# Two-layer decoder trunk on one Trainium2 core: the low parts of the weight splits of the attention and output stages in one VectorE operation per unit in place of two

## The chip, the cores and the metric

The kernel runs on one core of one Trainium2 chip, in one launch. The metric is the device time in microseconds of that core; lower is better. Beside the plain runs there is one profiled execution, whose trace is read here. Engine names in the rows: PE is TensorE (matrix products and transposes), PEld its weight loads, DVE is VectorE, ACT is ScalarE, POOL is GpSimd, SP is SyncE, which issues most DMAs.

## The reference, cut to what matters

The input is x, 256 tokens by 1024, in float32, and goes through two layers. Each layer computes:

```
h = RMSNorm(x);  proj = h @ w_in          # aq ak av | ix | bq bk bv | gates
ya = sparse attention: an indexer (4 heads) scores the keys, each query keeps its top 64, 8 heads of 64
yb = differential attention: 4 heads, softmax1 - lambda * softmax2, RMS norm per head
x  = x + ( sigmoid(gA) * (ya @ w_up_a) + sigmoid(gB) * (yb @ w_up_b) ) @ w_out
x  = x + SwiGLU(RMSNorm(x))               # hidden width 2816
```

The output is x, 256 by 1024, float32.

## The kernel before, in words

Every large product is made with float32 accuracy from three products of a shorter type: a matrix is split into a high part (`wh` for weights, made by ScalarE, a copy into the type fp32r) and a low part (`wl`, made by VectorE, the raw weight minus the high part), and `mm3` (lines 237 to 242) issues high times high, high times low and low times high. In the rows these are the lines L240, L241 (the one that reads `wl`) and L242.

Weights come in units of 512 rows by 512 columns or the like, packed so that a unit is a tile of 128 partitions by 2048 numbers in two halves of 1024 (the unit `ix` of the indexer has 2 x 648). A layer has 34 units ahead of its main feed-forward part: gA0, ix, ak, aq, av, bk, gA1, bq, bv, gB0, uA, gB1, uB with two each (names as in `BLOCKS`), four of `wo`, and four of the first two slabs `fi0` and `fi1`. A unit's raw tile has 4 buffers, its high and its low tile 4 each (`RAWS`, `RING`).

`ensure(k)` is called just ahead of the first product that uses unit k, and splits all units up to it by `split_half`, half by half: ScalarE writes 1024 numbers of `wh` (L149), VectorE 1024 of `wl` (L150). A wait of a matmul on `wl` is on the half that it reads. The first four units of layer 0 call `split_half` directly in `first_block`; the feed-forward units after `fi1` go through `high` and `low` (L197, L201), where the low part of a unit is already one operation of 2048.

The order of TensorE's and GpSimd's instructions is the program's own. VectorE's and ScalarE's instructions between `early.close()` and the feed-forward part are put in order by the framework's scheduler, which works from its own estimate of each instruction's length; within an engine they then run strictly in that order. So a change of one operation can move others of that engine.

Names needed below. After the products of a block, VectorE makes the rotated queries and keys of 128 tokens (`rope`, L455, L456, L458; for attention A's keys first L471, with the factor `ak00r` that GpSimd makes in L273 and L276), and TensorE transposes them, four or three transposes of 128x128 (L249), some ticks later: `ak00T` is layer 0, tokens 0 to 127. For the indexer (`idx_finish`) the third transpose of `ix01T` reads a piece that VectorE copies last (L497). The top-64 search (`indexer`, L529 and L530) is eight rounds of a maximum and a replacement for each 128 queries, `sc00m` and `sc01m` in layer 0 and `sc10m` and `sc11m` in layer 1, and fills VectorE between the other work.

Of the kernel before, what the change touches and what calls it, by code (L numbers as in the profile page):

```python
# [10 lines left out]
F32 = mybir.dt.float32  # L11
F32R = mybir.dt.float32r
I32 = mybir.dt.int32
AF = mybir.ActivationFunctionType
ALU = mybir.AluOpType
# [71 lines left out]
def tile_trunk(ctx, tc, x, angle, wpk, widx, gnorm, gbias, gqk, dlam, subln, const, out):  # L87
    nc = tc.nc
# [21 lines left out]
    seq, uidx, where = [], {}, {}  # L110
# [8 lines left out]
    held, ready, split = {}, [], [0]  # L119

    def raw_of(u):
        if u not in held:
            src, w = where[u]
            name = "raw" + "".join(str(a) for a in u)
            if u[2] == "22":
                raw = pp.tile([P, 2048], F32, name=name, tag="yT", bufs=1)
            else:
                raw = wp.tile([P, 2048], F32, name=name, tag="raw", bufs=RAWS)[:, :2 * w]
            for j in range(2):
                nc.sync.dma_start(raw[:, j * w:j * w + w], src[j])  # L130
            held[u] = raw
        return held[u]

    def new_ready(i):
        assert len(ready) == i
        ready.append([wp.tile([P, 2048], F32R, name=f"w{h}{i}", tag="w" + h, bufs=RING) for h in "hl"])
        return ready[i]

    def split_half(parts=1, between=None):
        n = split[0]  # L140
        split[0] += 1
        i, j = divmod(n, 2)
        hi, lo = ready[i] if j else new_ready(i)
        raw = raw_of(seq[i])
        w = raw.shape[-1] // 2
        m = w // parts
        for k in range(parts):
            c = slice(j * w + k * m, j * w + (k + 1) * m)
            nc.scalar.activation(hi[:, c], raw[:, c], AF.Copy)  # L149
            nc.vector.tensor_tensor(lo[:, c], raw[:, c], hi[:, c].bitcast(F32), ALU.subtract)  # L150
            if k == 0 and between:
                between()

    def ensure(k):
        while split[0] < 2 * min(k + 1, len(seq)):
            split_half()


    stage = {}
# [52 lines left out]
    def unit(l, name, i, kc, w):  # L212
        u = uidx[(l, name, i)]
        ensure(u)
        return [a[:, :kc * w].rearrange("p (a b) -> p a b", a=kc) for a in ready[u]]
# [882 lines left out]
```

## Time and profile before

| | us |
|---|---|
| median of 3 runs | 762.66 |
| lowest, highest | 762.52, 764.41 |
| profiled execution, its own time | 762.28 |
| span of its trace | 760.5 |
| TensorE busy | 751.3 (99%) |
| VectorE busy | 573.6 (75%) |
| ScalarE busy | 470.6 (62%) |
| GpSimd busy | 108.7 (14%) |

The profiled execution's own time is 1.78 us more than the span from its first to its last instruction. A row of the timeline gives the start in us from the span's start, the duration, the engine, line, operation and tiles, how many instructions are merged in it, and in brackets the idle time ahead of it with what ended it. Matmuls overlap: a 128x512 one is shown with 0.39 us, but the next starts about 0.23 us after it. A late start is therefore read from the distance between starts; the bracket shows the part of it in which the engine had nothing left in its pipeline.

### The profile page before, as it was taken

The numbers are of one execution on the slowest core, as the hardware profiler recorded it, in microseconds if no ns is written. First come the engines' busy times: TensorE is split into PE (matmuls) and PEld (weight loads), VectorE is DVE, ScalarE is ACT, GpSimd is POOL, SyncE is SP. The second block draws the span as 40 slices with busy tenths as digits, with TensorE's granted clock in tenths as the row PEclk, the third lists the DMA queues.
The fourth block names the chain that finished last, engine by engine and source line by source line (L and its number), as shares of the span: only waits on it lengthen the run. The fifth ranks groups of instructions, "written<-read, shape, count | busy, mean of one in ns | idle before, by whom it ended". The sixth has DMA issues, their size and how long they took to land.

```text
span 760.5 us, 10268 instructions
## 1 busy us (share of the span) xinstructions
PE 751.3 (99%) x3638; PEld 617.0 (81%) x3638; DVE 573.6 (75%) x885; ACT 470.6 (62%) x938; POOL 108.7 (14%) x135
## 2 busy tenths in 40 slices
PE   8999999999999999999999999999999999999998
PEld 5877888888888888888888787888888888888886
DVE  5999757768777777777768987667777877787673
ACT  5766597655665656656547676876546666565660
POOL 5741220010031100010001411200002010000100
PEclk9999999999999999999999999999999999999999
DMA  9744635436568888977746273443476599868921
GB/s 317 290 168 166 235 125 183 162 115 234 206 167 264 234 275 258 275 231 221 240 150 221 91 242 125 177 170 125 166 272 213 152 218 293 255 236 270 231 102 55
DMA packets 45061, 154.60 MB, mean 203 GB/s; under 512 B 5409, under 2 KB 6177, under 8 KB 45010
## 3 DMA queue, kind: packets, MB, share of 16 engines
q1 hardware_dynamic: 40320, 136.97, 49.1%
q0 software_dynamic: 4688, 16.98, 12.7%
q8 instruction: 28, 0.46, 0.2%
q14 instruction: 23, 0.19, 0.1%
q10 hardware_dynamic: 2, 0.00, 0.0%
HBM read 152.89 MB, written 1.05 MB: 202 GB/s over the span
## 4 chain that ended last, share of the span: by engine, by line
PE 90%; DVE 5%; ACT 1%; DMA 1%; POOL 1%; issue 1%; SPq 0%; ACTq 0%; DVEq 0%
PE fo L242 5%; PE fo L240 5%; PE fo L241 5%; PE fi L242 5%; PE fi L241 5%; PE fi L240 5%; PE qX L242 3%; PE qX L240 3%; PE qX L241 3%; PE gB L240 2%; PE gB L242 2%; PE wo L242 2%; PE gB L241 2%; PE wo L240 2%; PE wo L241 2%; PE gA L240 2%
## 5 line engine op out<-in xcount | busy, mean ns | idle before, releaser
L240 PE MATMUL fo<-wh,aTh 128*128 128x512 f32 (+1 forms) x100 | 38.2, 382 | 0.0
L241 PE MATMUL fo<-wl,aTh 128*128 128x512 f32 (+1 forms) x100 | 38.1, 381 | 0.0
L242 PE MATMUL fo<-wh,aTl 128*128 128x512 f32 (+1 forms) x100 | 38.1, 381 | 0.0
L197 ACT ACTIVATE wh<-raw1q 128x1024 fp32r<-128x1024 f32 (+1 forms) x24 | 30.0, 1268 | 8.3 <-DMA raw1q<-wpk 7.0
L197 ACT ACTIVATE wh<-raw0q 128x1024 fp32r<-128x1024 f32 (+1 forms) x24 | 30.0, 1268 | 8.1 <-DMA raw0q<-wpk 5.6
L201 DVE TENSOR_TENSOR wl<-raw0q,wh 128x2048 fp32r<-128x2048 f32 x15 | 34.2, 2284 | 0.6 <-ACT wh L197 0.6
L201 DVE TENSOR_TENSOR wl<-raw1q,wh 128x2048 fp32r<-128x2048 f32 x15 | 34.2, 2284 | 0.6 <-ACT wh L197 0.6
L240 PE MATMUL fo<-wh,aT 128*128 128x512 f32 x80 | 32.0, 400 | 0.0
L240 PE MATMUL fi<-wh,f0Th 128*128 128x512 f32 x80 | 31.9, 399 | 0.0
L240 PE MATMUL fi<-wh,f1Th 128*128 128x512 f32 x80 | 31.9, 399 | 0.0
L242 PE MATMUL fo<-wh,aT 128*128 128x512 f32 x80 | 31.3, 391 | 0.0
L242 PE MATMUL fi<-wh,f1Tl 128*128 128x512 f32 x80 | 31.2, 391 | 0.0
L242 PE MATMUL fi<-wh,f0Tl 128*128 128x512 f32 x80 | 31.2, 390 | 0.0
L241 PE MATMUL fo<-wl,aT 128*128 128x512 f32 x80 | 31.2, 390 | 0.0
L241 PE MATMUL fi<-wl,f0Th 128*128 128x512 f32 x80 | 31.2, 390 | 0.0
L241 PE MATMUL fi<-wl,f1Th 128*128 128x512 f32 x80 | 31.2, 390 | 0.0
L201 DVE TENSOR_TENSOR wl<-raw1fo,wh 128x2048 fp32r<-128x2048 f32 x11 | 25.1, 2285 | 3.4 <-ACT wh L197 3.4
L201 DVE TENSOR_TENSOR wl<-raw0fo,wh 128x2048 fp32r<-128x2048 f32 x11 | 25.1, 2285 | 3.4 <-ACT wh L197 3.4
L197 ACT ACTIVATE wh<-raw0fo 128x1024 fp32r<-128x1024 f32 x22 | 22.0, 1050 | 7.9 <-issue 4.0
L197 ACT ACTIVATE wh<-raw1fo 128x1024 fp32r<-128x1024 f32 x22 | 22.0, 1049 | 7.6 <-issue 4.1
L240 PE MATMUL wo<-wh,mTh 128*128 128x512 f32 x64 | 25.6, 400 | 0.0
L242 PE MATMUL wo<-wh,mTl 128*128 128x512 f32 x64 | 25.0, 391 | 0.0
(1050 smaller groups left out, 2490.2 us busy)
## 6 DMA issues: line engine op xcount, KB each, us to landing
raw0q<-wpk SPq DMA_DIRECT2D x24, 512.0 KB, 6.0
raw1q<-wpk SPq DMA_DIRECT2D x24, 512.0 KB, 5.6
raw0fo<-wpk SPq DMA_DIRECT2D x22, 512.0 KB, 6.2
raw1fo<-wpk SPq DMA_DIRECT2D x22, 512.0 KB, 6.0
raw0fi<-wpk SPq DMA_DIRECT2D x20, 512.0 KB, 4.2
raw1fi<-wpk SPq DMA_DIRECT2D x20, 512.0 KB, 4.4
raw0q<-wpk POOLq DMA_DIRECT2D x12, 512.0 KB, 6.8
raw1q<-wpk POOLq DMA_DIRECT2D x12, 512.0 KB, 7.6
```

The costliest lines, as they stand in the source:

```text
L197: nc.scalar.activation(hi[:, k * w:k * w + w], raw[:, k * w:k * w + w], AF.Copy)
L201: nc.vector.tensor_tensor(ready[n][1], stage.pop(("raw", n)), ready[n][0].bitcast(F32), ALU.subtract)
L240: nc.tensor.matmul(acc, lhsT=sh, rhs=mh, start=first, stop=False, skip_group_check=more)
L241: nc.tensor.matmul(acc, lhsT=sh, rhs=ml, start=False, stop=False, skip_group_check=more)
L242: nc.tensor.matmul(acc, lhsT=sl, rhs=mh, start=False, stop=last, skip_group_check=more)
```

## The change

`ensure` no longer calls `split_half`. For each unit it now makes both high halves on ScalarE, as before in two operations of 1024, and then the whole low part in one VectorE operation of 2048 (1296 for `ix`). It applies to all units that go through `ensure`: 30 in layer 0 and 34 in layer 1. `split_half` stays for the first four units.

```diff
     def ensure(k):
+
         while split[0] < 2 * min(k + 1, len(seq)):
-            split_half()
+            n = split[0] // 2
+            split[0] += 2
+            hi, lo = new_ready(n)
+            raw = raw_of(seq[n])
+            w = raw.shape[-1] // 2
+            for j in range(2):
+                nc.scalar.activation(hi[:, j * w:j * w + w], raw[:, j * w:j * w + w], AF.Copy)
+            nc.vector.tensor_tensor(lo[:, :2 * w], raw, hi[:, :2 * w].bitcast(F32), ALU.subtract)
```

TensorE's and GpSimd's instructions stand in the same order as before. In the built program after, lines behind `ensure` have numbers higher by 8 (L458 is L466, L497 is L505), and the new operation is L164. Three places of VectorE's queue follow.

Layer 0, indexer, tokens 128 to 255: `ix01q` is the rotated indexer query and key, `wl<-raw0aq` are the low parts of the two units of aq, `ak00xn` the first step of the keys of attention A. Before:

```order
L456 TENSOR_TENSOR ix01kb<-ix01q,sg_271 128x64
L150 TENSOR_TENSOR wl_579<-raw0aq_580,wh_578 128x1024
L458 TENSOR_TENSOR ix01q<-ix01q,ix01kb 128x64
L150 TENSOR_TENSOR wl_606<-raw0aq_607,wh_605 128x1024
L497 COPY ix01q<-ix01q 128x64
L150 TENSOR_TENSOR wl_606<-raw0aq_607,wh_605 128x1024
L471 TENSOR_TENSOR ak00xn<-ak_382,ak00r 128x512
```

And now:

```order
L464 TENSOR_TENSOR ix01kb<-ix01q,sg_271 128x64
L164 TENSOR_TENSOR wl_603<-raw0aq_604,wh_602 128x2048
L466 TENSOR_TENSOR ix01q<-ix01q,ix01kb 128x64
L479 TENSOR_TENSOR ak00xn<-ak_382,ak00r 128x512
L505 COPY ix01q<-ix01q 128x64
```

The whole of a unit's low part stands ahead of the addition into `ix01q`, and `ak00xn`, which reads `ak00r` from GpSimd, has moved ahead of the copy.

Layer 0, queries of attention A, tokens 128 to 255 (`aq01q`), with the low part of bk's first unit. Before:

```order
L150 TENSOR_TENSOR wl_798<-raw0bk_799,wh_797 128x1024
L529 MAX sc01m_558<-nb_159 128x8
L474 TENSOR_SCALAR rqaq_163<-rqaq_163 128x8
L455 TENSOR_TENSOR aq01q<-aq_642,cg_270 128x512
L530 MATCH_REPLACE nb_159<-sc01m_558,nb_159 128x256
```

And now:

```order
L164 TENSOR_TENSOR wl_792<-raw0bk_793,wh_791 128x2048
L537 MAX sc01m_556<-nb_159 128x8
L482 TENSOR_SCALAR rqaq_163<-rqaq_163 128x8
L463 TENSOR_TENSOR aq01q<-aq_638,cg_270 128x512
L538 MATCH_REPLACE nb_159<-sc01m_556,nb_159 128x256
```

The neighbours are the same; the operation ahead of them has 2048 numbers in place of 1024, and the second half no longer follows behind `aq01q`.

Layer 1, queries of attention A, tokens 0 to 127 (`aq10q`), with av's second unit. Before:

```order
L525 SCALAR_TENSOR_TENSOR nb_3447<-sc11r_3807,iw_3445,nb_3447 128x256
L531 TENSOR_SCALAR nb_3446<-nb_3446 128x128
L529 MAX sc11m_3811<-nb_3447 128x8
L533 TENSOR_TENSOR nb_3446<-nb_3446,cst 128x128
L530 MATCH_REPLACE nb_3447<-sc11m_3811,nb_3447 128x256
L150 TENSOR_TENSOR wl_3978<-raw1av_3979,wh_3977 128x1024
L529 MAX sc11m_3814<-nb_3447 128x8
L474 TENSOR_SCALAR rqaq_3450<-rqaq_3450 128x8
L455 TENSOR_TENSOR aq10q<-aq_3836,cg_2058 128x512
```

And now:

```order
L164 TENSOR_TENSOR wl_3939<-raw1av_3940,wh_3938 128x2048
L537 MAX sc10m_3669<-nb_3416 128x8
L537 MAX sc11m_3775<-nb_3417 128x8
L538 MATCH_REPLACE nb_3416<-sc10m_3669,nb_3416 128x128
L538 MATCH_REPLACE nb_3417<-sc11m_3775,nb_3417 128x256
L539 TENSOR_SCALAR nb_3416<-nb_3416 128x128
L537 MAX sc11m_3778<-nb_3417 128x8
L541 TENSOR_TENSOR nb_3416<-nb_3416,cst 128x128
L538 MATCH_REPLACE nb_3417<-sc11m_3778,nb_3417 128x256
L482 TENSOR_SCALAR rqaq_3420<-rqaq_3420 128x8
L463 TENSOR_TENSOR aq10q<-aq_3800,cg_2032 128x512
```

Between the key rotation of this layer (`ak11xn`) and `aq10q` there now stand the whole low part, and of the search rounds two more maxima of `sc10m`, one more replacement of `sc10m` and one more of `sc11m` than before.

## Rows read from the trace of the kernel before

**Rows 1.** The page's span and its part on the engines: busy us, share of the span, count of instructions.

```profile
span 760.5 us, 10268 instructions
PE 751.3 (99%) x3638; PEld 617.0 (81%) x3638; DVE 573.6 (75%) x885; ACT 470.6 (62%) x938; POOL 108.7 (14%) x135
```

**Rows 2.** The view by stretches of time: length, busy us (and instructions) of PE, PEld, DVE, ACT, POOL, then the granted clock, the share of DMA and GB/s.

```profile
38.00:76.00 38.00, 36.93 (x183) 29.37 (x182) 37.35 (x101) 25.38 (x81) 10.16 (x8) 1.00 0.45 168
76.00:380.00 304.00, 304.00 (x1469) 250.40 (x1467) 226.55 (x303) 191.68 (x346) 33.14 (x41) 1.00 0.67 214
```

**Rows 3.** The timeline of TensorE at five places: unit ak (L241 reads `wl`), the indexer's transposes, and the transposes of aq01, aq10 and bk10, each with the row ahead of it.

```profile
29.45 0.39 PE L241 MATMUL ak<-wl,a0Th 128*128 128x512 f32 x1
...
33.31 0.39 PE L240 MATMUL ak<-wh,a0Th 128*128 128x512 f32 x1
34.08 0.50 PE L241 MATMUL ak<-wl,a0Th 128*128 128x512 f32 x1 [0.39 <-DVE wl L150]
...
35.34 0.49 PE L249 MATMUL ix00T<-cst,ix00q 128*128 128x128 f32 x3
35.59 0.48 PE L240 MATMUL ak<-wh,a0Th 128*128 128x512 f32 x1
...
38.43 0.38 PE L249 MATMUL ix01T<-cst,ix01q 128*128 128x128 f32 x2
39.75 0.33 PE L249 MATMUL ix01T<-cst,ix01q 128*128 128x128 f32 x1 [0.94 <-DVE ix01q L497]
...
65.05 0.39 PE L242 MATMUL av<-wh,a0Tl 128*128 128x512 f32 x1
65.57 0.63 PE L249 MATMUL aq01T<-cst,aq01q 128*128 128x128 f32 x4
...
431.86 0.39 PE L242 MATMUL av<-wh,a1Tl 128*128 128x512 f32 x1
433.04 0.63 PE L249 MATMUL aq10T<-cst,aq10q 128*128 128x128 f32 x4 [0.79 <-DVE aq10q L458]
...
457.90 0.66 PE L249 MATMUL bk10T<-cst,bk10q 128*128 128x128 f32 x4 [0.21 <-DVE bk10q L458]
```

**Rows 4.** The timeline of VectorE in layer 0, from ak's low parts to the keys of attention A.

```profile
26.80 2.96 DVE L150 TENSOR_TENSOR wl<-raw0ak,wh 128x1024 fp32r<-128x1024 f32 x2
...
29.76 1.48 DVE L150 TENSOR_TENSOR wl<-raw0ak,wh 128x1024 fp32r<-128x1024 f32 x1
31.16 0.41 DVE L455 TENSOR_TENSOR ix00q<-ix,plain 128x256 f32<-128x256 f32 x1
...
32.81 1.22 DVE L150 TENSOR_TENSOR wl<-raw0ak,wh 128x1024 fp32r<-128x1024 f32 x1
33.95 0.22 DVE L458 TENSOR_TENSOR ix00q<-ix00q,ix00kb 128x64 f32<-128x64 f32 x1
...
34.20 0.20 DVE L497 COPY ix00q<-ix00q 128x64 f32<-128x64 f32 x1
...
39.50 0.19 DVE L497 COPY ix01q<-ix01q 128x64 f32<-128x64 f32 x1
...
41.15 0.69 DVE L471 TENSOR_TENSOR ak00xn<-ak,ak00r 128x512 f32<-128x512 f32 x1 [0.33 <-POOL ak00r L276]
```

**Rows 5.** The timeline of GpSimd: the power that makes the keys' factor, in layer 0 for both halves of the tokens and in layer 1 for the second.

```profile
38.51 2.60 POOL L276 TENSOR_TENSOR ak00r<-ak00r,mhalf 128x8 f32<-128x8 f32 x1
...
46.49 1.68 POOL L276 TENSOR_TENSOR ak01r<-ak01r,mhalf 128x8 f32<-128x8 f32 x1
...
419.32 2.73 POOL L276 TENSOR_TENSOR ak11r<-ak11r,mhalf 128x8 f32<-128x8 f32 x1
```

**Rows 6.** VectorE's groups with shapes kept apart (line, engine, operation, tiles, shape, count, busy us, mean ns of one, idle time ahead): a low part of 2048 and of 1024.

```profile
L201 DVE TENSOR_TENSOR wl<-raw0fi,wh 128x2048 fp32r<-128x2048 f32 x6 | 13.6, 2283 | 0.0
...
L150 DVE TENSOR_TENSOR wl<-raw1gB,wh 128x1024 fp32r<-128x1024 f32 x8 | 9.7, 1219 | 0.0
```

**Rows 7.** The timeline of VectorE at aq01 in layer 0.

```profile
61.30 1.21 DVE L150 TENSOR_TENSOR wl<-raw0bk,wh 128x1024 fp32r<-128x1024 f32 x1
...
64.76 0.67 DVE L458 TENSOR_TENSOR aq01q<-aq01q,aq01b 128x512 f32<-128x512 f32 x1
```

**Rows 8.** The timeline of VectorE in layer 1, from the keys' rotation to aq10.

```profile
422.08 0.69 DVE L471 TENSOR_TENSOR ak11xn<-ak,ak11r 128x512 f32<-128x512 f32 x1 [1.36 <-POOL ak11r L276]
...
425.21 0.28 DVE L529 MAX8 sc10m<-nb 128x8 f32<-128x128 f32 x1
...
430.96 0.41 DVE L530 MATCH_REPLACE8 nb<-sc11m,nb 128x256 f32<-128x256 f32 x1
...
432.22 0.67 DVE L458 TENSOR_TENSOR aq10q<-aq10q,aq10b 128x512 f32<-128x512 f32 x1
```

**Rows 9.** The timeline of VectorE at bk10 in layer 1.

```profile
457.16 0.68 DVE L458 TENSOR_TENSOR bk10q<-bk10q,bk10b 128x512 f32<-128x512 f32 x1
```

**Rows 10.** In layer 0's attention B: what ScalarE makes of a transpose (A013eT), and TensorE's use of it.

```profile
134.50 0.58 ACT L590 ACTIVATE A013eT<-A013T 128x512 f32<-128x512 f32 x1
...
136.77 1.00 PE L598 MATMUL Apv<-KV,A013eT 128*128 128x64 f32 x8
```

**Rows 11.** Two of TensorE's first matmuls of 128x512, behind the first transposes.

```profile
10.15 0.63 PE L242 MATMUL gA<-wh,a0Tl 128*128 128x512 f32 x1
10.58 0.63 PE L240 MATMUL gA<-wh,a0Th 128*128 128x512 f32 x1
```

## The prediction

> **What bounds the kernel now.** I read the page's engine part first: TensorE is busy 751.3 of 760.5 us [rows 1]. The stretches come next: from 76 to 380 us TensorE is busy 304.00 of 304.00, and from 38 to 76 us 36.93 of 38, where VectorE is busy 37.35 [rows 2]. So TensorE sets the end, and since its instructions and their order stay, the change is worth what it does to TensorE's waits. The timeline of TensorE shows where these stages wait for VectorE, and the distance of starts gives each wait: a 128x512 matmul is followed after 0.23 us (35.59 to 38.43 for twelve, the first with 0.1 extra) and a transpose after 0.11. The `wl` of ak costs 34.08-33.31-0.23 = 0.54 us; the third ix01T 39.75-38.43-0.22 = 1.10; aq01T 65.57-65.05-0.23 = 0.29; aq10T 433.04-431.86-0.23 = 0.95; bk10T has 0.21 idle in its bracket, and as the others' brackets lie 0.15 under the distance I take 0.36 [rows 3]. Together 3.24 us; that is all that a better VectorE could give back here.
>
> The reader is to see in VectorE's timeline what stood ahead of each of these: ix01q's copy at 39.50 ends 0.06 before the transpose starts, aq01q's addition at 65.43 (64.76+0.67), aq10q's at 432.89, bk10q's at 457.84 [rows 3, 4, 7 to 9]. All five waits are on what VectorE reaches late in its own queue.
>
> **What one operation costs.** A low part of 2048 takes 2.28 us, one of 1024 1.22 [rows 6]; back to back the second half starts 1.14 after the first (32.81 to the next operation at 33.95 [rows 4]), so two take 2.36 and one 2.28. The change removes 64 operations (30 units in layer 0, 34 in layer 1) and 64 x 0.08 = 5 us of VectorE's 573.6. That is no gain by itself, since TensorE is the bound. The low part's first half now comes later: it waits for both high halves, and a matmul on kc 0 or 1 waits for the whole. Where units lie well ahead of their use that is hidden; ak in layer 0 is the one that isn't. The price that matters is another: an operation behind a low part waits 2.2 us (2.28 less the overlap of 0.08) where it waited 1.14.
>
> [...]
>
> **Layer 0, ak and the indexer.** ak's first low part ends at 26.80+2.96-0.07 = 29.69; TensorE asks at 29.45 [rows 3, 4], so it waits 0.3. The second starts at 29.76 as before, under the same GpSimd load (its first half took 1.48 there), and ends about 29.76+1.40+1.22 = 32.4. That is before TensorE needs it, so the 0.54 go: -0.25 so far, and TensorE stands at ix00T at about 35.1 in place of 35.34. The six operations on ix00q, 31.16 to 32.81 before, now start at 32.3 and last 1.5 (0.15 of the old length was a wait that is over by then): 33.8. An `iw` and the addition make 34.05 (0.25, as from 33.95 to 34.20 [rows 4]). The first low part of aq now stands whole ahead of the copy: 34.05+2.2 = 36.25, and the copy ends at 36.45. The third ix00T could have gone at 35.3 and goes at 36.5, a new wait of 1.2.
>
> TensorE then does its twelve ak matmuls (2.84) and reaches the third ix01T at 36.6+2.84+0.2 = 39.65. VectorE's six operations on ix01q end at 36.35+1.5 = 37.85, the second low part of aq at 40.05, the addition at 40.2. Now `ak00xn` stands ahead of the copy (the first order block) and waits for GpSimd's factor. That came at 38.51+2.60 = 41.11 [rows 5] and comes 0.25 earlier with TensorE, 40.9. Then 0.65 for `ak00xn`, 0.2 for the copy: 41.75, against 39.50+0.19 = 39.69 before. TensorE goes on 2.05 us later than before. This is the net of layer 0's first part: +2.05. Bounds: if GpSimd takes the 1.68 that the same operation needs elsewhere [rows 5], `ak00xn` starts at 40.2 and it is +1.35; a further 0.5 above for the reverse.
>
> **Layer 0, aq01.** Behind this, VectorE is held by ak's second factor, which hangs on TensorE, so it is late by the same 2.05, less 0.3 for one maximum moved ahead and the saving. That keeps aq00T just free. Ahead of aq01q the low part of bk is 2048 instead of 1024 (second order block): +1.07. VectorE ends it at 65.43+1.75+1.07 = 68.25, plus 0.1 to the transpose; TensorE is there at 65.28+2.05 = 67.33. Wait 1.05 instead of 0.29: +0.75, between -0.29 (VectorE catches up) and +1.1. The second half that stood behind aq01q is gone, so VectorE is level again by attention A.
>
> **Layer 1, aq10.** ix11T has nearly 2 us left by the same working and stays free. From `ak11xn`, which waits for GpSimd until 422.08, aq10q's addition was 432.89 [rows 8]. In between now lie 1.07 more of low part, two maxima of sc10m (0.2 each, duration 0.28 less overlap), a replacement of sc10m (0.27 with its load) and one of sc11m (0.4): 2.15 (third order block). The transposes go at 435.2 in place of 433.04: +2.15, a wait of 3.1. If GpSimd's factor takes 1.68 in place of 2.73 [rows 5] it is +1.1. aq11T follows with the same content and 0.4 to spare.
>
> **Layer 1, bk10.** The addition into bk10q now stands ahead of bq's low part (1.22 before, 457.16 [rows 9]): the wait of 0.36 goes, -0.36.
>
> **Hidden parts.** ScalarE's work stays, with a few neighbours swapped; SP's load of a gate bias row passes behind one weight half, long before its use. In attention B, masks stand behind a whole low part, 1.1 to 1.4 us later. The nearest use is A013eT, ready 135.08 and used 136.77 [rows 10]: 1.69 in hand, of which I count 1.4 used. So 0, with up to 1 us if that cover goes. From `fi0` on nothing changes.
>
> **Sum.** 2.05+0.75+2.15-0.36 = +4.6 us on the profiled execution's 762.28: 766.9. That execution lies 0.4 under the median of 762.66 and inside the runs' range, so I leave it at 766.9.
>
> **Rivals.** (1) VectorE is the hidden bound, and 5 us less of it shorten the waits: all five vanish, -3.24, 759.0. For it speaks its 37.35 of 38 us; against it that in four of five places the order puts more ahead of what TensorE awaits. (2) Nearly nothing: GpSimd's powers run at 1.68, and VectorE catches up before aq01T: 1.35-0.29+1.1-0.36 = +1.8, 764.1. Against it: VectorE's load beside these powers stays. (3) The waits are longer than foreseen in two ways that add up: attention B loses its cover (+1), or TensorE's clock falls in the 3.1 us wait. [...] Ten matmuls at 0.43 in place of 0.23 cost 2 us; with both 769.9. Against it: none of the present waits, up to 1.1 us, lowered it.
>
> [...]
>
> **How the numbers follow.** My forecast has 0.70, (1) 0.04, (2) 0.12, (3) 0.14. The forecast's own range is 765.2 to 768.4. The range of 8 in 10 reaches down to near (2) and up to (3): 764.0 to 769.9. About 0.3%, or 2.3 us, is what a measurement here can tell from no change: faster 0.04, within 0.12, slower 0.84.
>
> **What would show it.** In the profile after: the low parts of these stages as 2048 with 2.28 us, TensorE waiting for the copies at ix00T (1.2) and ix01T (2.1), for aq01q (1.05) and aq10q (3.1), no wait at bk10T, and ak's wait moved to its first matmul on `wl`. `ak00xn` should start ahead of ix01q's copy with a wait for GpSimd. I am wrong if ix01T or aq10T waits no longer than before, if GpSimd's factor comes a microsecond earlier, or if waits appear in attention B or the output stage.

## The result and the profile after

The changed kernel took 770.78 us (median of 4 runs, 769.45 to 771.99), the kernel before 762.59 beside it: a ratio of 1.0100 with a 95% interval of 1.0087 to 1.0113. It is slower, as forecast, but by 8.2 us and not by 4.6, and the time lies 0.9 us above the predicted range. The profiled execution of after took 771.99, 9.71 more than that of before.

The page's head answers to [rows 1]: VectorE has 64 instructions and 3.6 us less, and the span is 9.7 us longer all the same.

```profile
span 770.2 us, 10173 instructions
PE 755.3 (98%) x3638; PEld 619.0 (80%) x3638; DVE 570.0 (74%) x821; ACT 470.4 (61%) x938; POOL 115.0 (15%) x135
```

The view by stretches (columns as in [rows 2]): TensorE works 1.2 us less in 38 to 76 us, and in 418 to 456 it idles 2.9 us and its granted clock falls. Between 442.5 and 445 the clock is 0.50.

```profile
38.00:76.00 38.00, 35.70 (x176) 28.40 (x177) 36.20 (x98) 24.40 (x91) 8.84 (x10) 1.00 0.45 167
...
418.00:456.00 38.00, 35.08 (x164) 27.95 (x163) 33.07 (x88) 24.15 (x83) 9.97 (x8) 0.96 0.39 142
442.50:445.00 2.50, 2.50 (x7) 1.93 (x6) 2.50 (x7) 0.00 (x0) 0.00 (x0) 0.50 0.22 36
```

The view of TensorE's waits (what waited, for what, us in total, times, longest) is the shortest way to the answer. Of these lines only aq10T and ix01T stand in the same view of before.

```profile
PE aq10T L257 <- DVE aq10q L466: 2.9, 1, 2.9
...
PE ix01T L257 <- DVE ix01q L505: 1.4, 1, 1.4
...
PE ix00T L257 <- DVE ix00q L505: 0.9, 1, 0.9
PE gA L250 <- DVE a1Tl L288: 0.8, 1, 0.8
...
PE gA L248 <- ACT a0Th L721: 0.6, 1, 0.6
PE B000T L257 <- DVE B000m L646: 0.5, 1, 0.5
PE aq01T L257 <- DVE aq01q L466: 0.4, 1, 0.4
PE B100T L257 <- DVE B100m L646: 0.3, 1, 0.3
PE aTT L257 <- DVE sg L911: 0.3, 1, 0.3
```

TensorE issues the same 3638 matmuls in the same order in both kernels, so each can be compared with itself. The table gives by how much TensorE's starts moved at each place (start after less start before; a step in this shift is time lost or won there). "Again" is a second profiled execution of the changed kernel, which took 770.52.

| place | forecast | after | again |
|---|---|---|---|
| start, up to 29 us | 0 | +2.59 | +0.95 |
| ak and indexer, layer 0, up to 44 us | +2.05 | +0.90 | +0.90 |
| aq01T | +0.75 | +0.29 | +0.24 |
| B000T (attention B, layer 0) | 0 | +0.70 | +0.72 |
| first aTT (feed-forward, layer 0) | 0 | +0.37 | +1.02 |
| a1Tl (start of layer 1) | 0 | +1.15 | +0.74 |
| aq10T | +2.15 | +2.13 | +2.11 |
| TensorE's clock behind aq10T | 0 | +1.58 | +1.51 |
| bk10T | -0.36 | -0.42 | -0.41 |
| B100T | 0 | +0.45 | +0.43 |
| sum | +4.6 | +9.7 | +8.2 |

The timeline of TensorE, for [rows 3]: the waits at ix00T, ix01T, aq01T and aq10T, and matmuls at 0.43 us apart behind the last of them (442.45 to 442.87), as at the kernel's start [rows 11]. bk10T has no wait.

```profile
38.56 0.33 PE L257 MATMUL ix00T<-cst,ix00q 128*128 128x128 f32 x1 [0.92 <-DVE ix00q L505]
...
43.21 0.33 PE L257 MATMUL ix01T<-cst,ix01q 128*128 128x128 f32 x1 [1.35 <-DVE ix01q L505]
...
441.17 0.63 PE L257 MATMUL aq10T<-cst,aq10q 128*128 128x128 f32 x4 [2.92 <-DVE aq10q L466]
...
442.45 0.63 PE L248 MATMUL av<-wh,a1Th 128*128 128x512 f32 x1
442.87 0.63 PE L249 MATMUL av<-wl,a1Th 128*128 128x512 f32 x1
...
467.26 0.61 PE L257 MATMUL bk10T<-cst,bk10q 128*128 128x128 f32 x4
```

The timeline of VectorE in layer 0, for [rows 4]: a whole low part of aq stands ahead of each copy, and `ak00xn` ahead of the second.

```profile
36.11 2.28 DVE L164 TENSOR_TENSOR wl<-raw0aq,wh 128x2048 fp32r<-128x2048 f32 x1
38.31 0.19 DVE L505 COPY ix00q<-ix00q 128x64 f32<-128x64 f32 x1
...
40.04 2.28 DVE L164 TENSOR_TENSOR wl<-raw0aq,wh 128x2048 fp32r<-128x2048 f32 x1
...
42.38 0.68 DVE L479 TENSOR_TENSOR ak00xn<-ak,ak00r 128x512 f32<-128x512 f32 x1
42.98 0.18 DVE L505 COPY ix01q<-ix01q 128x64 f32<-128x64 f32 x1
```

The timeline of GpSimd, for [rows 5]: an addition ahead of a power, on one number per partition, takes 2.04 us; the power that makes ak's first factor takes 1.68 in place of 2.60. It begins 0.34 us ahead of the low part at 40.04 in the fence above.

```profile
36.50 2.04 POOL L281 TENSOR_SCALAR ix01r<-ix01r 128x1 f32<-128x1 f32 x1 [1.49 <-ACT junk L498]
...
39.70 1.68 POOL L284 TENSOR_TENSOR ak00r<-ak00r,mhalf 128x8 f32<-128x8 f32 x1
```

In layer 1 the two operations that make ak11's factor traded their lengths. Before, the addition began under one half of a low part, that is while it ran (0.90 us), and the power under the other (2.73, [rows 5]):

```profile
418.33 0.90 POOL L273 TENSOR_SCALAR ak11r<-ak11r 128x8 f32<-128x8 f32 x1 [3.77 <-ACT junk L466]
```

Now the addition began under the whole low part (VectorE, 423.92 to 426.20) and the power came behind it:

```profile
424.33 1.98 POOL L281 TENSOR_SCALAR ak11r<-ak11r 128x8 f32<-128x8 f32 x1 [3.77 <-ACT junk L474]
426.40 1.67 POOL L284 TENSOR_TENSOR ak11r<-ak11r,mhalf 128x8 f32<-128x8 f32 x1
```

VectorE takes the factor at 428.10, which is 6.02 us later than the 422.08 of before, where the shift is 6.00: no time was won or lost there.

```profile
428.10 0.69 DVE L479 TENSOR_TENSOR ak11xn<-ak,ak11r 128x512 f32<-128x512 f32 x1 [1.63 <-POOL ak11r L284]
```

The timeline of VectorE in attention B of layer 0: the whole low part of uA stands ahead of the reciprocals, and `B000m`, which B000T reads, comes at 132.24. That low part waits 0.41 us for the high half.

```profile
129.57 2.29 DVE L164 TENSOR_TENSOR wl<-raw0uA,wh 128x2048 fp32r<-128x2048 f32 x1 [0.41 <-ACT wh L163]
131.78 0.22 DVE L643 RECIPROCAL Br<-Bs 128x2 f32<-128x2 f32 x2
...
132.24 0.34 DVE L646 SCALAR_TENSOR_TENSOR B000m<-B000m,B000c 128x128 f32<-128x128 f32 x1
```

Before, half a low part stood there, and `B000m` was ready 1.64 us ahead of B000T (126.63 and 128.27):

```profile
124.70 1.22 DVE L150 TENSOR_TENSOR wl<-raw0uA,wh 128x1024 fp32r<-128x1024 f32 x1
...
126.28 0.35 DVE L638 SCALAR_TENSOR_TENSOR B000m<-B000m,B000c 128x128 f32<-128x128 f32 x1
```

At the start of layer 1 VectorE stands on an addition that waits for a bias row by DMA, with a1Tl behind it. First SP and VectorE before, then after:

```profile
387.14 0.37 SPq L263 DMA_DIRECT2D gA10b<-gbias  x1
...
392.28 0.69 DVE L818 TENSOR_TENSOR gA<-gA,gA10b 128x512 f32<-128x512 f32 x1 [1.87 <-DMA gA10b<-gbias]
```

```profile
393.05 0.39 SPq L271 DMA_DIRECT2D gA10b<-gbias  x1
...
399.73 0.69 DVE L826 TENSOR_TENSOR gA<-gA,gA10b 128x512 f32<-128x512 f32 x1 [3.92 <-DMA gA10b<-gbias]
```

Less the shift of 4.91 at this place, the row is issued at 388.14 (1.0 later) and the addition runs at 394.82 (2.5 later). SP issues two halves of aq ahead of the row where it issued one, and the first of them 0.54 later, when the raw buffer comes free.

### The profile page after: what moved, and what is told of

Its sections match the earlier page's. It is cut to its first block, busy times and chain, and to the rows that moved or that the text cites. A ratio compares the mean times of both kernels' runs of the same rounds, so it can differ in the third digit from the quotient of the medians.

```text
span 770.2 us, 10173 instructions
## 1 busy us (share of the span) xinstructions
PE 755.3 (98%) x3638; PEld 619.0 (80%) x3638; DVE 570.0 (74%) x821; ACT 470.4 (61%) x938; POOL 115.0 (15%) x135
## 4 chain that ended last, share of the span: by engine, by line
PE 76%; DVE 9%; ACT 6%; POOL 4%; DMA 3%; issue 2%; SPq 0%; DVEq 0%; ACTq 0%; POOLq 0%
PE fo L250 5%; PE fo L248 5%; PE fo L249 5%; PE fi L250 4%; PE fi L248 4%; PE fi L249 4%; PE qX L250 3%; PE qX L249 3%; PE qX L248 3%; DVE wl L164 2%; PE gB L248 2%; ACT wh L163 2%; PE gB L250 2%; PE wo L250 2%; PE gB L249 2%
```

## The experiments

Each kernel ran beside the kernel before on the same chip, and ratios are to it. "Shift" is the measure of the table above, against the same profiled execution before. The intervals of several variants of the changed kernel overlap with its own, so what one place costs is read from the traces and not from the medians. Where a kernel makes some units by two operations again, the edit in `ensure` is this one, with a condition that is named:

```
         while split[0] < 2 * min(k + 1, len(seq)):
             n = split[0] // 2
+            if CONDITION:
+                split_half()
+                split_half()
+                continue
```

**One layer alone.** Condition `seq[n][0] == 1` (merged in layer 0 only) and `seq[n][0] == 0` (in layer 1 only).

> The merged operation in layer 0 alone; layer 1 keeps two operations per unit. Theory A: the loss is a sum of separate waits, each at its place, and the late first weights of the profiled run of the changed kernel (2.6 us before any changed instruction) are chance. From the shift of TensorE's starts between the two traces, layer 0's terms are ak -0.66, ix00T +1.08, ix01T +0.41, aq01T +0.26, B000T +0.66, the first aTT +0.26: +2.0, so about 764.6, with the start at 0 to 2.6 from run to run. In layer 1 nothing is shifted and TensorE's clock stays at 1.00. Rival B: the late start comes with the change itself; then about 767.2 here, with the first gA matmul on weights at 10.2 us as in the changed kernel and not at 9.2. Rival C: the loss is spread evenly over the operations: half of it, 766.7.

Measured: 766.05 us, ratio 1.0040 (1.0028 to 1.0052). Profiled with a start 2.49 late and 2.30 of loss behind it, all of it ahead of 250 us: +0.91 to 44 us, aq01T +0.25, B000T +0.7, aTT +0.4. From there on the shift is constant. The time alone would fit rival C as well, and the first matmul on weights, at 10.44, fits rival B, which the control of the start below answers.

> The merged operation in layer 1 alone. Theory A: layer 1's terms alone, a1Tl +1.03 (a gate bias row that lands later), aq10T +2.13, the clock behind it +1.72, bk10T -0.38, B100T +0.42: +4.9, so about 767.5; layer 0 as before. If the clock's fall needs the rest of the change, 765.8. Rival B (the start belongs to the change): about 770.1. Rival C: 766.7.

Measured: 766.74 us, ratio 1.0046 (1.0034 to 1.0058), runs from 764.92 to 767.27. The profiled run is the fastest: shift 0 up to 220 us, aq10T +2.11, bk10T -0.42, B100T +0.5, but only +0.2 at a1Tl and no loss behind aq10T. With a wait of the same length (TensorE's timeline) the granted clock stayed at 1.00 (the stretch behind it, columns as in [rows 2]):

```profile
435.62 0.63 PE L261 MATMUL aq10T<-cst,aq10q 128*128 128x128 f32 x4 [2.90 <-DVE aq10q L470]
```

```profile
435.60:445.00 9.40, 9.38 (x50) 7.68 (x51) 9.33 (x19) 4.40 (x6) 0.00 (x0) 1.00 0.36 127
```

So the losses are separate and stay in their layers (theory A), and two of them, the clock and the bias row, differ from run to run.

**One unit ahead of aq10q.** The changed kernel with condition `seq[n] == (1, "av", 1)`.

> The changed kernel with one unit, the second of av in layer 1, made by two operations again, so that only one half of it stands ahead of aq10q; the other steps of the reordering by the scheduler (maxima and replacements ahead of aq10q) stay. My sum has 1.07 us for the longer operation of the 2.15 at aq10T. Theory A1: the wait falls from 3.08 to about 2.0 and TensorE's clock still falls behind it: 769.7. A2: the clock stays at its higher level behind a wait of 2.0: about 768.0. Rival: the reordering or GpSimd's factor sets aq10q and the operation's length is hidden: no change against the changed kernel, 770.8.

Measured: 768.97 us, ratio 1.0080 (1.0067 to 1.0093). aq10T shifts by 1.04 in place of 2.13: 1.09 of it is the longer operation and the rest the reordering, as the prediction had it (1.07 and 1.08). But aq11T lost 0.99, since the second half now stands ahead of its content. The clock stayed up behind both waits, of 2.0 and 1.0 (a mean of 1.000 in the profiled execution, 0.999 or 1.000 in the other three runs), and that is the gain.

**The clock.** The record has the mean granted clock of every execution over its span: 0.999 or 1.000 in all 45 of the kernel before beside these experiments, 0.996 to 0.998 in all eight of the changed kernel. First the changed kernel with matmuls in TensorE's wait:

```
             b = bank(name + "T")
+            if name == "aq10":
+                xh = NA["T"][0]
+                for _ in range(11):
+                    nc.tensor.matmul(b, lhsT=xh[:, 0, :P], rhs=xh[:, 0:2, :].rearrange("p a b -> p (a b)"), start=True, stop=True)
             transposes(b, q, range(4))
```

> The changed kernel with eleven matmuls of 128x512 more, whose result is overwritten, issued by TensorE in the wait ahead of aq10T (2.5 us of the 3.08). Theory A: the granted clock falls behind aq10T because TensorE is idle there; with the idle time filled it stays at 1.00, aq10T starts as before in its place and 1.7 us go: 769.1. Rival: the clock falls for another reason (the load of the whole chip at that time, a passing throttle): 770.8 or more. The added matmuls delay nothing, since they end before aq10q is there.

Measured: 769.24 us, ratio 1.0085 (1.0069 to 1.0102), 1.5 under the changed kernel's median; runs from 767.92 to 772.16, with a mean clock of 0.999 or 1.000 in all but the longest (0.998). aq10T shifts by 2.04 and behind it nothing is lost. In TensorE's timeline the filling ends 0.33 us ahead of the transposes, and the matmuls behind are 0.23 apart:

```profile
437.20 2.65 PE L491 MATMUL aq10T<-a1Th 128*128 128x512 f32 x11
440.19 0.66 PE L257 MATMUL aq10T<-cst,aq10q 128*128 128x128 f32 x4 [0.33 <-DVE aq10q L466]
...
440.91 0.39 PE L249 MATMUL av<-wl,a1Th 128*128 128x512 f32 x1
441.14 0.40 PE L250 MATMUL av<-wh,a1Tl 128*128 128x512 f32 x1
```

Then the same filling in the kernel that is merged in layer 1 alone.

> The merged operation in layer 1 alone, with eleven overwritten matmuls in the wait ahead of aq10T. Without them this kernel took 764.92 in its profiled execution, where TensorE's clock stayed up behind a wait of 3.1 us and the first weights came on time, and 766.1 to 767.3 in the other four. Theory A: in those four the clock fell behind aq10T (1.7 us); then all five runs here lie at 764.6 to 765.2. Rival: the four were late at the start, which the added matmuls don't touch; then they spread up to 767 again.

Measured: 765.77 us (765.55 to 766.95), ratio 1.0045 (1.0033 to 1.0058). Both expectations miss: four runs lie within 0.5 us, but above 765.2, and the fifth, the profiled one, started 1.1 late. My level came from a run without the loss at a1Tl; here a1Tl costs 0.99. The mean granted clock says more of the other runs of layer 1 alone: 0.998 and 0.997 in the two longest (767.27 and 767.18), 0.999 in those of 766.07 and 766.74, and 0.999 or 1.000 in all five here. So the clock can have made two of the four longer, and not the other two.

Last, the wait without the change: two VectorE operations more ahead of aq10T in the kernel before.

```
         rope(heads(q, 8), heads(src, 8), cg[:, i, :], sg[:, i, :], 8, name)
+        if name == "aq10":
+            for _ in range(2):
+                nc.vector.tensor_tensor(q, q, q, ALU.max)
```

> The kernel before, with two VectorE operations more (the maximum of aq10q with itself) behind the addition into aq10q, so that aq10T waits about 2.9 us (0.95 and 1.94) without any merged operation. Theory A: idle time of TensorE of this length can by itself put its clock to half speed for some of the following matmuls: where it does, +1.9 and +1.7, about 766.4; where not (as in the profiled execution with the merged operation in layer 1 alone), 764.7; the five runs then lie in two groups. Rival: the clock's fall needs the changed kernel's load; then no run above 765.5 and no matmul of 0.43 behind aq10T.

Measured: 765.63 us (764.46 to 766.34), ratio 1.0037 (1.0023 to 1.0050); the runs don't fall into two clear groups by time, but the shortest has a mean clock of 1.000 and the other four 0.997 or 0.998. In the profiled one aq10T shifts by 1.94, the matmuls behind it start 0.43 apart at a granted clock of 0.50 (436.0 to 437.7 us), and 1.4 us more are lost before the spacing is 0.23 again:

```profile
434.74 1.09 PE L249 MATMUL aq10T<-cst,aq10q 128*128 128x128 f32 x4 [2.73 <-DVE aq10q L479]
...
436.06 0.63 PE L241 MATMUL av<-wl,a1Th 128*128 128x512 f32 x1
436.48 0.63 PE L242 MATMUL av<-wh,a1Tl 128*128 128x512 f32 x1
```

So the wait alone is enough, with no merged operation, and in the two profiled executions with the idle time filled the clock didn't fall (a mean of 0.999 in both, and 1.00 from 440.5 to 445.0 us in the changed kernel).

**The bias row.** The changed kernel with this row in a buffer of its own, loaded at the kernel's start:

```
+            soon["gA", 0] = cp.tile([P, 512], F32, name="gA10b")
+            nc.sync.dma_start(soon["gA", 0], gbias[l + 1:l + 2, 0:512].to_broadcast([P, 512]))
...
-                gb[g, c] = row(gbias, l, 2 * (g == "gB") + c, f"{g}{l}{c}b")
+                gb[g, c] = soon.pop((g, c), None) if l else None
+                gb[g, c] = gb[g, c] or row(gbias, l, 2 * (g == "gB") + c, f"{g}{l}{c}b")
```

> The changed kernel with the first gate bias row of layer 1 (gA10b) in a buffer of its own, loaded at the start of the kernel; the instructions of all engines but the order of SP's loads stay. Theory A: the wait of 0.92 us on a1Tl in layer 1 comes from this row, which lands later because SP issues it behind one weight half more and issues that half later (the ring buffer comes free when the whole low part of ix has read it). Then the addition into gA no longer waits, the shift at a1Tl is 0 in place of +0.9, and the rest stays: 769.9, where the start and the clock behind aq10T may move it. Rival: a1Tl is late because VectorE's longer operations hold it; then the shift at a1Tl stays +0.9 and 770.8.

Measured: 769.41 us, ratio 1.0087 (1.0073 to 1.0100). The shift is 3.13 at 380 us and 3.14 at 400: the loss at a1Tl is gone and was the row's. The clock fell behind aq10T (+1.6): the matmuls are 0.43 apart there, and the mean clock of this execution is 0.997. Of the five runs, the two with a mean clock of 0.999 took 768.1, the three with 0.995 to 0.997 took 769.4 to 770.7.

**The start.** Low parts in two operations, only written in another order in the source:

```
-            nc.vector.tensor_tensor(lo[:, :2 * w], raw, hi[:, :2 * w].bitcast(F32), ALU.subtract)
+            for j in range(2):
+                c = slice(j * w, j * w + w)
+                nc.vector.tensor_tensor(lo[:, c], raw[:, c], hi[:, c].bitcast(F32), ALU.subtract)
```

> A control for the start: low parts in two operations as before, with the source rewritten so that both are written behind both high halves. Every engine's order of instructions is then the one of the kernel before. Theory A (the late first weights are chance of each loaded program): same as before within 0.3%, 762.6, and some runs up to 2.6 us late at the first matmul on weights. Rival B (they belong to the changed instructions): no run later than before's, the first matmul on weights at 9.2.

Measured: 763.19 us, ratio 1.0007 (0.9998 to 1.0016). With the instructions of before in the same order, the first matmul on weights came at 9.98 and the shift was 1.62 at 29 us:

```profile
9.98 0.79 PE L250 MATMUL gA<-wh,a0Th 128*128 128x512 f32 x1 [0.37 <-ACT a0Th L723]
```

So a late start isn't due to the changed instructions; ScalarE waited 2.12 us for the first weights to land, where it had waited 0.79. Here it dropped to 0.97 at 36 us, since ak's wait of 0.54 vanished. That wait, for which I had credited the change with 0.25, isn't there in every run of two operations either.

> The changed kernel once more, unchanged. Theory A: the shift of TensorE's first matmuls on weights (2.56 us in the profile shown) is chance from run to run and now lies elsewhere between 0 and 2.6; behind it the same waits at the same places (ix00T 1.1, ix01T 1.5, aq01T 0.56, B000T 0.66, a1Tl 0.6 to 0.9, aq10T 3.1), and the clock behind aq10T falls (1.7) or doesn't: 767.7 to 772. Rival: the first matmul comes at 10.2 us again, and then the late start belongs to this program.

Measured: 770.44 us (769.97 to 771.07), ratio 1.0091 (1.0074 to 1.0108). The last column of the table is its profile: the start lies elsewhere (+0.95), the steps that hang on VectorE's order repeat within 0.05, and aTT and a1Tl, which hang on small loads, differ by 0.4 to 0.65. Its start lost time in another way: the first matmul on weights came at 9.06, 0.09 earlier than before, but eight distances of 0.43 between starts followed, where before it was three.

```profile
9.06 0.78 PE L248 MATMUL gA<-wh,a0Th 128*128 128x512 f32 x1
...
12.62 0.63 PE L250 MATMUL gA<-wh,a0Tl 128*128 128x512 f32 x1
13.05 0.53 PE L248 MATMUL gA<-wh,a0Th 128*128 128x512 f32 x1
```

**Can the gain be had without the loss?** Merged only where the table shows a gain; condition `not (seq[n][0] == 0 and seq[n][1] == "ak" or seq[n][0] == 1 and seq[n][1] == "bq")`.

> The merged operation only where the ledger of the changed kernel shows a gain: the keys' unit ak in layer 0 (its wait of 0.54 on the low part went) and bq in layer 1 (the wait of 0.38 at bk10T went); all else in two operations. Theory A: ak -0.66, ix00T unchanged, since only 1.14 of low part stand ahead of its copy, bk10T -0.38; ix01T takes back 0 to 0.66, because VectorE's work ahead of it is the same and TensorE is earlier: 761.6 to 762.3. Rival: ix00T waits now, because half a low part of aq has moved ahead of its copy: 762.7 or more.

Measured: 764.68 us, ratio 1.0027 (1.0017 to 1.0038): slower than before. ak's merged units alone moved the maxima of the indexer ahead of the addition into aq00q, which before ran at 58.46. In VectorE's and TensorE's timelines:

```profile
60.40 0.68 DVE L470 TENSOR_TENSOR aq00q<-aq00q,aq00b 128x512 f32<-128x512 f32 x1
...
61.23 0.63 PE L261 MATMUL aq00T<-cst,aq00q 128*128 128x128 f32 x4 [1.49 <-DVE aq00q L470]
```

That is +1.65 at a place that had no wait; bk10T gained its 0.4, the first aTT lost 0.6 and A102eT 0.9. The rival's wait at ix00T came too (+0.75), and its 762.7 or more held, but aq00T stood in neither of my two cases.

The other way round, the units at fault in layer 0 in two operations: condition `seq[n][:2] == (0, "aq") or seq[n] == (0, "bk", 0)`, and then the same with `(1, "av", 1)` and the early bias row.

> The changed kernel with three units of layer 0 in two operations again, those whose long operation stands ahead of a row that TensorE waited for: both units of aq (ahead of the copies into ix00q and ix01q) and the first of bk (ahead of aq01q). Theory A, by the working of the prediction: ix00T's new wait of 1.08 goes (1.14 less ahead of the copy), ix01T gains 0.5 to 0.6 (ak00xn is behind its copy again), aq01T 0.25 to 0.55: the shift of TensorE's starts at 70 us is 2.0 us less than in the changed kernel with the same start, the rest stays: about 768.8. Rival: the reordering of the maxima around it brings a new wait of its own, as ak alone did at aq00T (1.65): then aq00T waits over 1 us and the time stays near 770.

> The same, and in layer 1 the second unit of av in two operations and the gate bias row loaded early: all the repairs together. Theory A, the losses are separate and add up: of the changed kernel's 7.1 us without its late start, 2.0 go in layer 0, 0.95 at a1Tl, 1.7 of the clock; at aq10T and aq11T together 0.1: 2.3 us over the profiled execution before, 764.6, and up to 2 more by a late start. B000T and B100T still wait (0.66 and 0.42). Rival: repaired places hand their wait on to the next one; then it stays above 767.

Measured: 769.39 us, ratio 1.0082 (1.0070 to 1.0095), and 767.30, ratio 1.0059 (1.0046 to 1.0072). With the three units split the new waits at ix00T and ix01T went, but aq00T waits (+0.88): 1.2 of the 2.0 us came back, the rest passed on. With all repairs the row's loss and the clock's are gone (a mean clock of 1.000 in all five runs), yet of 4.54 us in the profile, with a start on time, most lies at places I thought settled: aq00T +0.47, the first attention +0.45 at A003eT, and +1.0 each at aq10T and aq11T, where I had 0.1 together. B000T's +0.7 was expected to stay. The rival's half of the expectation holds: repaired places hand their wait on.

## Why the prediction was right and wrong

**Right.** TensorE sets the end, and VectorE's saving (3.6 us in the profile, 5 forecast) bought nothing. aq10T came as worked out: 2.15 forecast, 2.13 and 2.11 measured, and the experiment on av splits it into operation and order as the text did. Part of that was luck: the sum rests on a factor of GpSimd that comes no earlier, with +1.1 if the power takes 1.68. The power did take 1.67, but the addition ahead of it took 1.98 in place of 0.90, and the two cancelled. bk10T won its 0.36; the kernel with ak and bq alone merged won it too, but so did the delayed kernel before, where TensorE came later and bq stayed in two operations. In the changed kernel either would do. ix00T's new wait was forecast at 1.2 and was 1.08. Rival (1) is refuted, and rival (2) with its +1.8 too, although the powers of both layers ran at the length that it asked for.

**The sum.** Less its start, the second profile of the changed kernel is 7.3 us longer than before, where the forecast had 4.6. Too much was forecast for ak and the indexer (1.15) and for aq01T (0.5); missing were attention B (1.15), the first aTT (1.0), the bias row (0.7) and the clock (1.5).

**Mis-sized: layer 0's first part and aq01.** The net of +2.05 was +0.90. The step that failed is "that came at 38.51+2.60 = 41.11": GpSimd's power took 1.68, the lower of my two durations, and `ak00xn` started at 42.38 without a wait for it. What had stretched it to 2.60 was not the stage's load but one low part under which it began. In the traces of before and after, GpSimd's additions that began under a low part ended 0.08 to 0.17 us after it, all 24; in the lines above, 36.50+2.04 = 38.54 stands against 36.11+2.28 = 38.39. The powers on 128x8 that began under one ended 1.52 to 1.53 after it, all six, and took 2.47 to 2.73 before and 3.54 to 3.55 in after. With the order changed ak00r's power began 0.34 ahead of the next low part and kept its 1.68, although that low part then ran beside it.

With 1.68 the prediction's own bound is +1.35; the rest is ak, which won 0.66 and not 0.25, chiefly since the 0.3 at its first matmul on `wl` didn't come. Of the 0.66, the wait of 0.54 also went without the change, as the control of the start shows. aq01T follows: ahead of bk's low part VectorE was 0.1 late (63.97, less 2.59, against 61.30 before) and not 1.75, so 0.75 became 0.29.

The merged operation lasts 2.28 us in place of 1.22, so a GpSimd addition that begins under it can take longer: 2.04 and 1.98 us in the fences above, where the longest in before took 1.06. That speaks against this change. What ties the two engines the rows don't show. The low part at 40.04 began beside a running power and took its usual 2.28. GpSimd's busy time rose from 108.7 to 115.0.

**Wrong: "attention B ... So 0".** I had searched for the nearest use among what ScalarE makes [rows 10] and took A013eT. TensorE also reads what VectorE makes itself, and B000m and B100m came 0.4 to 0.7 too late for it: +0.7 and +0.45. That the low part of uA ahead of them does it is read off the queue; no run has that unit alone in two operations. Rival (3) had attention B at +1, at another row.

**Wrong: the bias row "passes behind one weight half, long before its use".** The row was already the last to arrive before: VectorE waited 1.87 us for it at 392.28. It cost 0.74 to 1.15, shown by taking the load away from that place. The first aTT is alike: in after, as before, VectorE stands on a product that waits for a load by DMA (`dl`, 2.54 us before, 2.64 after, 3.14 again). That its landing sets aTT was read off, not tested.

**Given too little: the clock.** Rival (3) priced it at 2 us with both its parts at 0.14 of chance, and argued that "none of the present waits, up to 1.1 us, lowered it". No row of before has a wait of 3.1, so this could not count against it. Its ten matmuls were my estimate, and its 0.43 the distance at the kernel's start [rows 11], where the view of before gives a granted clock of 1.00 (9.00 to 14.00 us); no row of before shows a wait that brings this distance about. In after, seven distances behind aq10T were 0.43, at a granted clock of 0.50 (442.2 to 445.6 us). The loss there was 1.58 in after and 1.51 in the second profile of it, and the mean clocks of 0.996 to 0.998 speak for a fall in all eight executions of the changed kernel. Of six profiled executions that left aq10T waiting about 3 us, four show the fall (after, again, the early row, and the delayed kernel before) and two don't (layer 1 alone, and the three units split). What decides between them stays open.

**Not foreseen: the start.** 0.95 and 2.59 us of the two profiles of after are lost before any changed instruction runs. In the first, the first weights landed later (the first matmul came 1.1 late) and eleven distances between starts were 0.43, where before it was three; in the second only these distances were more. Both differ between runs of unchanged orders too. Without it, the loss is 7.1 and 7.3 us.

## What to carry to other kernels

An operation merged from two is priced by what waits behind it on its engine: a consumer that stood between the two halves is late by the second half (1.09 us at aq10T), whether or not the engine is busy on average. Where a scheduler sets the order, one merged operation reorders what follows, and the order was worth as much as the length here (1.04 us at aq10T); compare the rows for every tile that the bound engine reads from this one, and for every load that a queued instruction waits for. Once a new wait is several times the old ones (here 3.1 us against at most 1.1), price the clock with it: 1.4 to 1.6 us in four of six profiled executions.

## What the runs showed of the hardware

- A GpSimd addition that begins under a low part of VectorE ends 0.08 to 0.17 us after it (24 of 24 in before and after): on 128x1 it took 0.24 us with VectorE idle (at 5.38 in before) and 2.04 beside a 128x2048 low part. A power on 128x8 that begins under one ends 1.52 to 1.53 us after it (6 of 6); one that began 0.34 us ahead of a low part took its 1.68 (at 39.70 in after).
- Behind the same idle time of TensorE, 2.7 to 2.9 us in the wait's bracket, matmuls of 128x512 were 0.43 us apart in four profiled executions and 0.23 in two. The granted clock of such a stretch was 0.50 in after and in the delayed kernel before, and 1.00 in layer 1 alone and with the three units split. Where it fell, 1.4 to 1.6 us were lost.
- The first matmul on weights started between 9.06 (again) and 10.44 us (layer 0 alone) in the fourteen profiled executions, behind the same program text; it came at 9.15 in before and 10.23 in after. Behind it 2 to 11 distances between starts were about 0.43 us (three in before, eleven in after), the spacing seen behind aq10T at a granted clock of 0.50; here the view gives 1.00 (9.00 to 14.00 us in before, 10.00 to 15.50 in after), so what makes them is not shown. In after, a start 1.1 late and eight more of these distances cost 2.6.
